# Half tile's expert rows join the joint query and are gathered from the late gather's buffers, on a one-core Trainium2 decoder step

## The chip, the cores and the metric

The kernel runs on one core of a Trainium2 chip, as one program in one launch. The metric is device time in microseconds, the median of several executions. Engines are named as in the profile: PE multiplies matrices (PEld loads its weights), DVE, ACT and POOL work elementwise, SP only issues DMAs. POOL and ACT issue DMAs too; every gather from a table by indices is issued by POOL.

## The reference, cut to what matters

One decoder layer runs over 1024 prompt tokens and 64 sample tokens with the same weights: a norm, one input projection, two token mixers (a retention and an RWKV-7 scan), an output projection, then PEER, an expert mixer, then a gated per-layer embedding and a final norm. PEER is the part that the change touches. Each token queries 8 heads with two halves of 128 keys each, keeps 16 of each half, adds them to candidates, keeps 16 of these, and reads 16 rows per head from two tables of 16384 experts:

```
q = (xb @ wq).reshape(PEER_BLOCK, PEER_HEADS, 2, PEER_DKEY // 2)
s = jnp.einsum('phcd,hcnd->phcn', q, keys).astype(jnp.float32)
sv, si = lax.top_k(s, PEER_TOPK)
cand = sv[:, :, 0, :, None] + sv[:, :, 1, None, :]
cv, ci = lax.top_k(cand.reshape(...), PEER_TOPK)
e = (take(si[:, :, 0], ci // PEER_TOPK) * PEER_NKEYS + take(si[:, :, 1], ci % PEER_TOPK))
gsm = jax.nn.softmax(cv, axis=-1)
hval = jnp.einsum('pd,phkd->phk', xb, u_tab[e])
act = (jax.nn.gelu(hval, approximate=False) * gsm).astype(xb.dtype)
return jnp.einsum('phk,phkd->pd', act, v_tab[e])
```

## The kernel before, in words

The 1088 tokens are cut into nine tiles: tiles 0 to 7 hold 128 prompt tokens each, tile 8 the 64 sample tokens, so it is half a tile. PEER is done in two ways.

*Gathered tiles.* For tiles 0, 1, 8, 2 and 3 each token's 128 rows of both tables are fetched. `gather` issues one indirect DMA per column of the expert list `eid`, 128 rows of 4 KB, 512 KB (L1154 on POOL). First come the rows of the u table: DVE multiplies a row with the token and sums (L1168). Then gelu and the softmax weight on ACT and DVE, then the rows of the v table: DVE adds weight times row to `gacc` in PSUM (L1182). A full tile takes 128 + 128 calls. Tile 8's two halves of the expert list are laid on 128 partitions, so it takes 64 + 64. `gacc` is one buffer, so gathers follow one another. Early gathers (list `E0`: 0, 1, 8) use a ring of eight or nine row buffers in the pool `early`; late gathers (list `G1`: 2, 3) use five buffers named `grow` in the pool `gat`, which is laid out after the pools of the mixers and of `early` are closed and over their memory.

*Dense tiles.* For tiles 4 to 7 (`G2`, 512 tokens) all 16384 experts are multiplied: `hidden` (L1312 and on) makes u times x for 128 blocks of experts, 24 matmuls each, with operands split into a high and a low part on ACT and POOL (tiles `uh`, `ul`); `gates` writes one-hot weights (`oh`, `pwt`, `wst`); `act` multiplies them; `dense` multiplies with v (`vraw`, `vh`, `vl`, `py`). The first 80 hidden blocks are stored in DRAM while the gates are made, the other 48 are used at once (`dense_fused`), then the stored ones are read back (`dense_stored`).

The stages in order are: input projections; mixers of all tiles (`group_b`, order 1, 8, 2 to 7 after tile 0), with `c_rows` behind each (output projection, residual, norm: the tile's row `xd` that PEER reads); the joint query `c_query` for tiles of `G1` and `G2` (16 blocks of weights, for each a matmul per part, scores, and `pick`, five DVE instructions per tile that keep 16 of 128 scores); the hidden stage; fused dense; stored dense; and `ple`, the final stage, tile by tile, in the order `E0 + G2 + G1`. Tile 3's final stage adds `gacc` directly (L1446).

Beside the mixers runs the generator `early`: tile 0's query of its own (`early_query`, 16 weight blocks of 512 KB, matmuls `epq` at L1232 and L1235, 16 picks, then `topk`; for tiles 1 and 8 the scores go to DRAM and back before the picks) and its gather; tile 1's query and gather; and, stepped along with tile 1's gather once tile 8's row is there, tile 8's query; then tile 8's gather. `topk` turns picks into the expert list: sums of candidates, 8 rounds of maxima and index searches, and 8 rounds of a difference on POOL (`eq`, L1102) and a reduction on DVE (`ef`, L1104).

The order on each engine is made by the framework's scheduler when the program is built: it places ready instructions by the order in which the code emits them, with its own estimate of times, and each engine then runs its list strictly in that order, waiting on semaphores. A gather call whose buffer is not free holds up what stands behind it on POOL.

Of the kernel before, what the change touches and what calls it, by code (L numbers as in the profile page):

```python
# [9 lines left out]
F32 = mybir.dt.float32  # L10
# [3 lines left out]
U32 = mybir.dt.uint32  # L14
AF = mybir.ActivationFunctionType
# [156 lines left out]
PWS = 4  # L172
NPRE = 80
NF = 4
TK1 = {2: 1, 3: 4}
GEB = 2
GHB = 2
WQ = 32
# [1 line left out]
WB = 2  # L180
AB = 8
CRING = 4
E0 = [0, 1, 8]
G1 = [2, 3]
DW = 4
LW = 3
CN = 4
# [9 lines left out]
G2 = [4, 5, 6, 7]  # L197
# [3 lines left out]
QB = 4  # L201
SB = 3
EB = 150
SIZE = {t: (64 if t == 8 else 128) for t in range(9)}


def spans(tiles):

    e = [sum(SIZE[t] for t in tiles[:i]) for i in range(len(tiles) + 1)]
    return dict(zip(tiles, e)), e[-1]  # L210
# [8 lines left out]
class K:  # L219
# [797 lines left out]
    def c_query(self, wp, da, parts):  # L1017

        nc, I = self.nc, self.I
        for hc in range(16):  # L1020
            kT = wp.tile([128, 128], F32, name="keysT")
            nc.sync.dma_start(kT, I['keysT'][:, hc])
            raw = da.tile([128, 8, 128], F32, name="wqr", tag="uraw", bufs=UB)
            nc.sync.dma_start(raw, I['wq'][hc])
            wh = da.tile([128, 8, 128], F32R, name="wqh", tag="uh", bufs=DW)
            wl = da.tile([128, 8, 128], F32R, name="wql", tag="ul", bufs=LW)
            self.split(wh, wl, raw, "g")
            for tiles, x in parts:
                off, n = spans(tiles)
                s = wp.tile([128, len(tiles), 128], F32, name=f"ss{tiles[0]}", bufs=SB)  # L1030
                p = self.ps("pq", "b")
                self.mm3(p[:, :n], lambda k: wh[:, k, :], lambda k: wl[:, k, :], lambda k: x[0][:, k], lambda k: x[1][:, k], 8)
                qT = wp.tile([128, n], F32, name=f"qT{tiles[0]}", bufs=1)
                nc.scalar.activation(qT, p[:, :n], AF.Copy)
                p = self.ps("psc", "a")
                for i, t in enumerate(tiles):
                    nc.tensor.matmul(p[:SIZE[t], i * 128:i * 128 + 128], qT[:, off[t]:off[t] + SIZE[t]], kT, start=True, stop=True)
                nc.scalar.activation(s, p[:, :len(tiles) * 128].rearrange("p (t k) -> p t k", k=128), AF.Copy)
                for i, t in enumerate(tiles):
                    self.pick(self.found[t], hc, s[:, i], 128)  # L1040
            yield

    def pick(self, found, hc, s, n):
# [8 lines left out]
    def topk(self, tp, t, s=None, tags={}, ce=None):  # L1052
        nc = self.nc
        n = SIZE[t]
        if s is None:
            sv, si = self.found[t]
        else:
            sv = tp.tile([128, 16, 16], F32, name="sv")
# [47 lines left out]
        if t in G2:  # L1106
            gsm = self.gsm[t] = tp.tile([128, 128], F32, name="gsm", bufs=2)
            self.e12[t] = tp.tile([128, 2, 128], F32, name="e12", bufs=2)
        elif t == 8:
            gsm = tp.tile([128, 128], F32, name="gsm8", tag="cf")  # L1110
        else:
            gsm = self.gsm[t]
        ex = tp.tile([128, 8, 16], F32, name="ex")
# [137 lines left out]
    def early(self, wp):  # L1251

        rows = ("V", "V", "Wq", "Wq", "Wq", "Wq", "W", "xy")
        self.wide = True
        yield from self.early_query(wp, E0[0], "Wq", QB, (("W",), ("xy",)))
        g = self.gather(wp, E0[0], rows, acc=self.acc)
        while E0[1] not in self.rowed:
            next(g, None)
            yield
        self.wide = False  # L1260
        for i, _ in enumerate(self.early_query(wp, E0[1], "Wq", QB, ("Wq", "xT"))):
            if i % 3 == 0:
                next(g, None)
            yield
        yield from g
        g = self.gather(wp, E0[1], rows, acc=self.acc)
        q = None
        for i, _ in enumerate(g):
            yield
            if E0[2] in self.rowed and q is None:  # L1270
                q = self.early_query(wp, E0[2], "Wq", QB, ("Wq", "xT"))
            if q and i % 1 == 0:
                next(q, None)
        for _ in q:
            yield
        self.wide = False
        yield from self.gather(wp, E0[2], rows + ("xT",), acc=self.acc)

    def gates(self, wp, t, extra):
        nc = self.nc  # L1280
# [201 lines left out]
    def build(self):  # L1482
        PS = bass.MemoryType.PSUM
        run = lambda g: [None for _ in g]
        sb = lambda name, es, **kw: self.pool(name, es=es, reuse_waits="tile", **kw)
        with self.es:
# [32 lines left out]
            for _ in a:  # L1519
                for _ in range(IE):  # L1520
# [7 lines left out]
            parts = [G1, G2]  # L1528
            self.layout(cq, [(f"ss{g[0]}", [128, len(g), 128], F32, SB) for g in parts] +
                        [(f"qT{g[0]}", [128, spans(g)[1]], F32, 1) for g in parts])  # L1530
            c1 = sb("cx1", ew, side="right")
            x1 = self.rows_of(c1, G1)
            cx = sb("cx2", ex)
# [1 line left out]
            da = sb("dna", eg, bufs=2)  # L1535
            self.layout(da, [("uh", [128, 8, 128], F32R, DW), ("ul", [128, 8, 128], F32R, LW), ("uraw", [128, 8, 128], F32, UB), ("spare", [128, 8, 128], F32, 1)])
            tp = sb("tk", et)
            self.found = {t: (tp.tile([128, 16, 16], F32, name=f"sv{t}"), tp.tile([128, 16, 16], U32, name=f"si{t}")) for t in G1 + G2}
            self.e12 = {}
            n3 = spans(G2[:-1])[1]  # L1540
            query = self.c_query(cq, da, [(G1, x1), (G2, x)])
# [16 lines left out]
            run(ahead)  # L1558
            run(last)
            run(query)  # L1560
            run(early)
            ew.close()
            ee.close()
# [10 lines left out]
            with ExitStack() as e:  # L1574
# [9 lines left out]
                for i, t in enumerate(G2 + [None]):  # L1584
# [8 lines left out]
                    gate = self.gates(gw, t, da) if t is not None else gate  # L1593
                    for t in G1:
                        if i == TK1[t]:
                            run(self.topk(tp, t))
                            run(self.behind(self.gather(gp, t, acc=acc), PG))
            et.close()
            self.first = True
# [31 lines left out]
```

## Time and profile before

| | |
|---|---|
| runs shown | 3690.5, 3701.82, 3702.95 us (median 3701.82) |
| profiled execution | 3682.12 us, its span 3680.3 us |
| busy over the span | PE 89%, PEld 74%, DVE 78%, ACT 33%, POOL 64% |
| gather calls | 1152, 604 MB of the 1075 MB moved |
| gather of tile 8 | 1863 to 2271 us |
| gather of tile 2, of tile 3 | 2271 to 2934 us, 2934 to 3649 us |

The page's first part gives busy time by engine. Its second part cuts the span into 40 slices with the clock that PE was granted and the busy share of the DMA engines. A table of stretches gives the same for any stretch, and can be restricted to one tile's instructions, which counts the gather calls. A row of a group reads: line, engine, operation, what is written from what, shapes, count, then busy time and mean duration in ns, then the engine's idle time just before and what ended it. A row of the timeline reads: start, duration, engine, line, operation, names, count.

The names in the rows: `Z` is the start of a mixer tile's triangular solve, which PE carries on with the products trz, pG and pZG; `wql` is the low part of a weight block of the joint query, `ul` that of a hidden block, `vl` that of a dense block; `nrs` and `frs` are the two norms of a tile's final stage.

### The profile page before, as it was taken

The page shows a single profiled execution, that of the slowest core. Times are in us where ns is not written, and L with a number is a line of the kernel's source. Part 1 is how long each engine was busy: PE and PEld are TensorE (multiplying, and loading weights), DVE is VectorE, ACT ScalarE, POOL GpSimd, SP SyncE. Part 2 cuts the span into 40 slices and gives each one's busy share as a digit, 9 for nine tenths or more (in the row PEclk, how much of TensorE's full clock was granted, in tenths as well). Part 3 has the DMA queues.
Part 4 walks back from the last instruction along what each step waited for, and adds up shares of the span by engine and source line. Part 5 has one row for each costly group of instructions (what it writes and reads, how often), then busy time and mean ns, then how long its engine had stood idle before and what let it go on. Part 6 is the DMA issues. An engine that isn't in the chain of part 4 may idle for free. (4 is left out here: it accounts for less than half of the span.)

```text
span 3680.3 us, 52362 instructions
## 1 busy us (share of the span) xinstructions
PE 3268.2 (89%) x17749; PEld 2715.5 (74%) x17749; DVE 2857.6 (78%) x5655; ACT 1218.4 (33%) x2259; POOL 2345.1 (64%) x2068
## 2 busy tenths in 40 slices
PE   8798996887968888876989999999999998899988
PEld 7697995654846667655877887887888877667766
DVE  4544689897797886688997999776777787778887
ACT  4233221111211211112333887773333333333322
POOL 5352677554355654436468777768888878887752
PEclk9798996666968885877999999999999999999999
DMA  7257599889858887878678988999999999999974
GB/s 263 86 192 244 200 350 316 277 300 309 280 187 308 311 298 238 300 252 295 206 261 310 324 311 287 345 350 355 342 346 339 332 364 353 369 361 365 340 246 167
DMA packets 423558, 1074.69 MB, mean 292 GB/s; under 512 B 46267, under 2 KB 143289, under 8 KB 418618
## 3 DMA queue, kind: packets, MB, share of 16 engines
q0 software_dynamic: 165888, 604.05, 45.9%
q1 hardware_dynamic: 202670, 377.02, 30.9%
q10 hardware_dynamic: 54732, 90.26, 6.6%
q8 instruction: 141, 2.31, 0.3%
q14 instruction: 127, 1.04, 0.1%
HBM read 980.93 MB, written 90.18 MB: 291 GB/s over the span
## 5 line engine op out<-in xcount | busy, mean ns | idle before, releaser
L1154 POOL DMA_INDIRECT grow<-in_pv,eid x576 | 569.5, 989 | 534.4 <-DVE gacc L1182 299.0
L1154 POOL DMA_INDIRECT grow<-in_pu,eid x576 | 564.2, 979 | 343.1 <-DVE grow L1168 203.2
L1168 DVE SCALAR_TENSOR_TENSOR grow<-grow,gacc 128x1024 f32<-128x1024 f32 x576 | 690.2, 1212 | 116.7 <-DMA grow<-in_pu,eid 114.9
L1182 DVE SCALAR_TENSOR_TENSOR gacc<-grow,ac,gacc 128x1024 f32<-128x1024 f32 x571 | 731.1, 1280 | 33.2 <-DMA grow<-in_pv,eid 28.2
L1353 PE MATMUL py<-ah,vh 128*128 128x512 f32 x1024 | 406.8, 398 | 32.2 <-ACT vh L304 32.2
L333 PE MATMUL ph<-cx,uh 128*128 128x512 f32 x1024 | 406.8, 397 | 7.2 <-DVE al L306 4.6
L334 PE MATMUL ph<-cx,uh 128*128 128x512 f32 x1024 | 405.0, 396 | 0.0
L1354 PE MATMUL py<-al,vh 128*128 128x512 f32 x1024 | 404.7, 395 | 0.0
L308 POOL TENSOR_TENSOR vl<-vraw,vh 128x640 fp32r<-128x640 f32 (+1 forms) x224 | 325.9, 1461 | 39.9 <-ACT vh L304 30.2
L308 POOL TENSOR_TENSOR ul<-uraw,uh 128x1024 fp32r<-128x1024 f32 x128 | 308.1, 2407 | 49.1 <-ACT uh L304 21.0
L1356 PE MATMUL py<-ah,vl 128*128 128x512 f32 x1024 | 272.3, 397 | 13.9 <-POOL vl L308 13.8
L336 PE MATMUL ph<-cx,ul 128*128 128x512 f32 x1024 | 263.4, 395 | 0.0
L1353 PEld LDWEIGHTS py<-ah,vh 128*128 128x128 f32 x1024 | 196.0, 191 | 82.0 <-ACT vh L304 40.3
L304 ACT ACTIVATE vh<-vraw 128x640 fp32r<-128x640 f32 (+1 forms) x224 | 154.8, 692 | 274.3 <-DMA vraw<-in_pvd 95.9
L1356 PEld LDWEIGHTS py<-ah,vl 128*128 128x128 f32 x1024 | 192.3, 189 | 63.3 <-POOL vl L308 21.7
L333 PEld LDWEIGHTS ph<-cx,uh 128*128 128x128 f32 x1024 | 194.8, 190 | 47.0 <-DVE al L306 5.0
L1360 DVE TENSOR_TENSOR yT<-yT,py 128x512 f32<-128x512 f32 x216 | 147.5, 684 | 102.1 <-PE py L1356 101.0
L1354 PEld LDWEIGHTS py<-al,vh 128*128 128x128 f32 x1024 | 195.8, 191 | 41.1
L334 PEld LDWEIGHTS ph<-cx,uh 128*128 128x128 f32 x1024 | 194.5, 190 | 38.5
L336 PEld LDWEIGHTS ph<-cx,ul 128*128 128x128 f32 x1024 | 191.3, 189 | 38.2
L304 ACT ACTIVATE uh<-uraw 128x1024 fp32r<-128x1024 f32 x128 | 135.0, 1056 | 162.0 <-DMA uraw<-in_puT 109.3
L1297 DVE TENSOR_TENSOR oh<-csta,pit 128x1024 f32<-128x1024 f32 x128 | 153.6, 1210 | 27.5 <-ACT oh L1299 17.9
(402 smaller groups left out, 7247.9 us busy)
## 6 DMA issues: line engine op xcount, KB each, us to landing
uraw<-in_puT SPq DMA_DIRECT2D x128, 512.0 KB, 4.2
vraw<-in_pvd SPq DMA_DIRECT2D x128, 320.0 KB, 7.2
cw<-in_w_out SPq DMA_DIRECT2D x128, 256.0 KB, 5.9
wd<-wst ACTq DMA_DIRECT2D x28, 1024.0 KB, 12.3
wt<-wd SPq DMA_DIRECT2D x64, 448.0 KB, 6.8
wraw<-in_w_ret SPq DMA_DIRECT2D x48, 512.0 KB, 4.2
ewq<-in_wq SPq DMA_DIRECT2D x48, 512.0 KB, 5.0
vraw<-in_pvd SPq DMA_DIRECT2D x96, 256.0 KB, 5.4
```

The source lines that it names most:

```text
L304: nc.scalar.activation(hi, src, AF.Copy)
L308: nc.gpsimd.tensor_tensor(lo, src, hi.bitcast(F32), op=OP.subtract)
L333: mm(out, lh(k), rh(k), start=first and k == 0, stop=False)
L334: mm(out, *((ll(k), rh(k)) if right else (lh(k), rl(k))), start=False, stop=False)
L336: mm(out, *((lh(k), rl(k)) if right else (ll(k), rh(k))), start=False, stop=last and k == nk - 1)
L1154: nc.gpsimd.indirect_dma_start(out=g, out_offset=None, in_=src, in_offset=bass.IndirectOffsetOnAxis(ap=self.eid[t][:, j:j + 1], axis=0))
L1168: nc.vector.scalar_tensor_tensor(g[:, c], g[:, c], 1.0, x[:, c], op0=OP.mult, op1=OP.mult, accum_out=hv[:, i, j:j + 1])
L1182: nc.vector.scalar_tensor_tensor(y[:, c], g[:, c], ac[:, j:j + 1], y[:, c], op0=OP.mult, op1=OP.add)
L1297: nc.vector.tensor_tensor(oh, io, p[:, 0:2, s + b:s + b + 4, None].to_broadcast([128, 2, 4, 128]), op=OP.is_equal)
L1353: nc.tensor.matmul(p, vh[:, b, :], ah, start=b == 0, stop=False)
L1354: nc.tensor.matmul(p, vh[:, b, :], al, start=False, stop=False)
L1356: nc.tensor.matmul(p, vl[:, b, :], ah, start=False, stop=b == nb - 1)
```

## The change

The lists change: tile 8 leaves `E0` and goes to the front of `G1`. So `early` ends with tile 1's gather and holds no query for tile 8; the joint query's first part has 320 columns (tiles 8, 2, 3) where it had 256, with one more copy of scores on ACT and 16 more picks of 64 partitions on DVE; `topk` of tile 8 is emitted right behind the joint query, ahead of what is left of `early`; tile 8's gather is emitted in the hidden stage's first round (`TK1` has 8: 0), behind the first 16 hidden blocks, and takes the five buffers of `gat`. Tile 8's picks are kept in a small pool of their own that closes with the mixers' pools. In the final stage tile 8 comes after tiles 4 to 7.

```diff
-TK1 = {2: 1, 3: 4}
+TK1 = {8: 0, 2: 1, 3: 4}
-E0 = [0, 1, 8]
-G1 = [2, 3]
+E0 = [0, 1]
+G1 = [8, 2, 3]
...
-                nc.scalar.activation(s, p[:, :len(tiles) * 128].rearrange("p (t k) -> p t k", k=128), AF.Copy)
+                m = len([t for t in tiles if t == 8])
+                for t in tiles[:m]:
+                    nc.scalar.activation(s[:64, 0], p[:64, :128], AF.Copy)
+                nc.scalar.activation(s[:, m:], p[:, m * 128:len(tiles) * 128].rearrange("p (t k) -> p t k", k=128), AF.Copy)
                 for i, t in enumerate(tiles):
-                    self.pick(self.found[t], hc, s[:, i], 128)
+                    self.pick(self.found[t], hc, s[:, i], SIZE[t])
...
-            gsm = tp.tile([128, 128], F32, name="gsm8", tag="cf")
+            gsm = tp.tile([128, 128], F32, name="gsm8", tag="gsm", bufs=2)
...
         g = self.gather(wp, E0[1], rows, acc=self.acc)
-        q = None
-        for i, _ in enumerate(g):
-            yield
-            if E0[2] in self.rowed and q is None:
-                q = self.early_query(wp, E0[2], "Wq", QB, ("Wq", "xT"))
-            if q and i % 1 == 0:
-                next(q, None)
-        for _ in q:
-            yield
         self.wide = False
-        yield from self.gather(wp, E0[2], rows + ("xT",), acc=self.acc)
+        yield from g
...
+            cf = sb("cf8", ew, side="right")
...
-            self.found = {t: (tp.tile([128, 16, 16], F32, name=f"sv{t}"), tp.tile([128, 16, 16], U32, name=f"si{t}")) for t in G1 + G2}
+            self.found = {}
+            for t in G1 + G2:
+                fp = cf if t == 8 else tp
+                self.found[t] = (fp.tile([128, 16, 16], F32, name=f"sv{t}"), fp.tile([128, 16, 16], U32, name=f"si{t}"))
...
             run(query)
+            run(self.topk(tp, 8))
             run(early)
...
                         if i == TK1[t]:
-                            run(self.topk(tp, t))
+                            if t != 8:
+                                run(self.topk(tp, t))
                             run(self.behind(self.gather(gp, t, acc=acc), PG))
```

The scheduler moves the instructions. How many gather calls stand in POOL's list between marks is, before and in the change:

| between | before | change |
|---|---|---|
| Z of the last mixer tile but one, and Z of the last | 50 | 34 |
| Z of the last mixer tile, and the joint query's first wql | 43 | 39 |
| first wql, first ul | 44 | 44 |
| first ul, first vl | 204 | 188 |
| first vl, last ul | 187 | 189 |
| last ul, last vl | 201 | 200 |
| behind the last vl | 45 | 80 |

Three places of the lists follow. The first is PE's list in the solve of the last mixer tile but one, where tile 8's query (`epq`) stood. Before:

```order
L850 MATMUL trz<-csta,Z 128x128 x4
L855 MATMUL pG<-Z,N 128x64 x4
L862 MATMUL pZG<-G_12122,Tt_12115 128x64 x3
L1232 MATMUL epq<-exT,ewq 128x64 x8
L458 MATMUL tr<-csta,qv 128x128 x4
L862 MATMUL pZG<-G_12122,Tt_12115 128x64
L862 MATMUL pZG<-G_12176,Tt_12169 128x64 x4
L1235 MATMUL epq<-ekT,eqT 64x128
L1232 MATMUL epq<-exT,ewq 128x64 x8
```

In the change, the same solve:

```order
L850 MATMUL trz<-csta,Z 128x128 x4
L458 MATMUL tr<-csta,qv 128x128 x4
L855 MATMUL pG<-Z,N 128x64 x4
L458 MATMUL tr<-csta,qv 128x128 x4
L862 MATMUL pZG<-G_11643,Tt_11636 128x64 x4
L466 MATMUL pin<-qkT 128x128 x8
L862 MATMUL pZG<-G_11669,Tt_11662 128x64 x4
L850 MATMUL trz<-csta,Z 128x128 x4
```

The query's 144 matmuls are gone from between the solve's steps, and the next tile's first products stand there.

The second place is POOL's list at the end of the joint query. `eid_65` is tile 1's expert list, `eid_66` tile 8's. Before:

```order
L308 TENSOR_TENSOR wql<-wqr,wqh 128x1024
L1154 DMA grow<-in_pv,eid_65 128x1024 x2
L308 TENSOR_TENSOR wql<-wqr,wqh 128x1024
L1154 DMA grow<-in_pu,eid_66 128x1024 x3
L308 TENSOR_TENSOR ul<-uraw,uh 128x1024
L1154 DMA grow<-in_pu,eid_66 128x1024 x5
L308 TENSOR_TENSOR ul<-uraw,uh 128x1024
```

In the change, the last calls of tile 1 and the first of tile 8 stand some rows further on, behind tile 8's top-k and the 14th ul:

```order
L1157 DMA grow<-in_pv,eid_65 128x1024
L1105 TENSOR_TENSOR eq<-eid,cf 64x800
L308 TENSOR_TENSOR ul<-uraw,uh 128x1024
L1105 TENSOR_TENSOR eq<-eid,cf 64x800
L308 TENSOR_TENSOR ul<-uraw,uh 128x1024
L1105 TENSOR_TENSOR eq<-eid,cf 64x800
...
L1082 TENSOR_TENSOR eid<-sf 128x8x3
L1085 TENSOR_TENSOR eid<-sf 128x8x6
L1089 TENSOR_TENSOR eid<-sf 128x8x8
L1157 DMA grow<-in_pu,eid_66 128x1024 x5
L308 TENSOR_TENSOR ul<-uraw,uh 128x1024
```

Tile 8's gather followed tile 1's without a gap; now its top-k and the start of tile 4's stand between, with five hidden blocks and no call.

The third place is the end of POOL's list, with the last gather calls of tile 3 (`eid_68`). Before:

```order
L299 TENSOR_TENSOR nrs<-nrs,halves 128x1
L298 TENSOR_SCALAR frs<-fssq 128x1
L1154 DMA grow<-in_pv,eid_68 128x1024
L299 TENSOR_TENSOR frs<-frs,halves 128x1
L1154 DMA grow<-in_pv,eid_68 128x1024
L298 TENSOR_SCALAR frs<-fssq 128x1
L299 TENSOR_TENSOR frs<-frs,halves 128x1
L298 TENSOR_SCALAR nrs<-nssq 128x1
L299 TENSOR_TENSOR nrs<-nrs,halves 128x1
```

In the change:

```order
L298 TENSOR_SCALAR frs<-fssq 128x1
L1157 DMA grow<-in_pv,eid_68 128x1024
L299 TENSOR_TENSOR frs<-frs,halves 128x1
L1157 DMA grow<-in_pv,eid_68 128x1024 x26
L298 TENSOR_SCALAR nrs<-nssq 128x1
L299 TENSOR_TENSOR nrs<-nrs,halves 128x1
L298 TENSOR_SCALAR frs<-fssq 128x1
L299 TENSOR_TENSOR frs<-frs,halves 128x1
```

The calls ended among the norms of the final stage; now 26 stand in a row behind the norms of all other tiles, and only tile 3's two norms come after.

## The prediction

> **What bounds the kernel now.** I read first the table of stretches (busy time of each engine, granted clock, DMA share), cut where the work changes: two ordinary mixer tiles, the tile beside which tile 8's query runs, the rest of the mixers, the joint query, the hidden stage with its gates, fused dense, stored dense, and the final stage in two pieces.
>
> ```profile
> core 0: us, PE busy (x) PEld busy (x) DVE busy (x) ACT busy (x) POOL busy (x), PEclk, DMA share, GB/s
> 1205.00:1305.00 100.00, 84.25 (x513) 65.81 (x514) 84.18 (x161) 18.48 (x37) 58.71 (x58) 0.86 0.88 309
> 1305.00:1407.00 102.00, 88.45 (x509) 70.82 (x509) 81.18 (x157) 18.51 (x37) 55.93 (x57) 0.78 0.82 289
> 1407.00:1589.00 182.00, 149.53 (x812) 122.68 (x812) 120.61 (x269) 29.88 (x74) 72.22 (x71) 0.70 0.75 253
> 1589.00:1708.00 119.00, 91.11 (x476) 67.33 (x474) 93.53 (x177) 19.97 (x35) 54.26 (x60) 0.77 0.87 305
> 1708.00:1860.00 152.00, 145.30 (x880) 129.52 (x881) 147.67 (x635) 47.38 (x79) 89.01 (x67) 0.97 0.68 221
> 1860.00:2502.00 642.00, 604.67 (x3124) 512.50 (x3123) 541.43 (x1182) 431.87 (x870) 486.88 (x386) 0.98 0.88 318
> 2502.00:2953.00 451.00, 451.00 (x1978) 372.30 (x1977) 340.51 (x452) 142.43 (x212) 386.15 (x312) 1.00 0.96 341
> 2953.00:3511.00 558.00, 511.88 (x2146) 408.26 (x2145) 442.68 (x722) 202.71 (x333) 438.63 (x366) 0.97 0.99 355
> 3511.00:3649.00 138.00, 128.29 (x585) 101.42 (x584) 121.95 (x147) 34.94 (x67) 67.72 (x74) 0.95 0.72 240
> 3649.00:3680.00 31.00, 20.95 (x92) 16.14 (x91) 13.84 (x21) 6.22 (x11) 2.23 (x6) 0.95 0.13 51
> ```
>
> The bound changes along the span. The mixers go by a chain over PE and DVE; the joint query by DVE (147.67 of 152 us) with PE close behind; the hidden stage and fused dense by PE (604.67 of 642; 451 of 451); stored dense by DMA (0.99). The last stretch tells who ends the program:
>
> ```profile
> 3647.27 1.28 DVE L1182 SCALAR_TENSOR_TENSOR gacc<-grow,ac,gacc 128x1024 f32<-128x1024 f32 x1
> ...
> 3650.39 1.21 DVE L1446 TENSOR_TENSOR ph<-ph,gacc 128x1024 f32<-128x1024 f32 x1
> ...
> 3659.29 1.42 DVE L1479 SCALAR_TENSOR_TENSOR fin<-ph,frs,row_norm_final 128x512 f32<-128x512 f32 x2 [1.15 <-POOL frs L299]
> ...
> 3675.67 1.41 DVE L1479 SCALAR_TENSOR_TENSOR fin<-ph,frs,row_norm_final 128x512 f32<-128x512 f32 x2 [2.19 <-POOL frs L299]
> ```
>
> The last gathered row of tile 3 is added at 3648.55; its final stage begins at 3650.39 and ends the program; the tile before it is done at 3660.7. So PE's stages and the gather arrive together. Time saved before the dense stages is kept only if the gather arrives as much earlier. I therefore count gather calls per stretch, and compare with where the new order puts them.
>
> ```profile
> core 0: us, POOL busy (x), PEclk, DMA share, GB/s
> 1305.00:1407.00 102.00, 39.04 (x40) 0.78 0.82 289
> 1407.00:1589.00 182.00, 50.59 (x51) 0.70 0.75 253
> 1589.00:1708.00 119.00, 42.14 (x44) 0.77 0.87 305
> 1708.00:1860.00 152.00, 42.39 (x44) 0.97 0.68 221
> 1860.00:2502.00 642.00, 194.41 (x205) 0.98 0.88 318
> 2502.00:2953.00 451.00, 178.54 (x188) 1.00 0.96 341
> 2953.00:3511.00 558.00, 192.68 (x202) 0.97 0.99 355
> 3511.00:3649.00 138.00, 50.38 (x45) 0.95 0.72 240
> ```
>
> By POOL's new order the same stretches hold 34 calls (tile with the query; 50 in the old order), 39 (43), 44 (44), 188 (204), 189 (187), 200 (201), and after the last vl split 80 where 45 stood. PE's stages keep their density of calls; what the shorter mixers and the later start of tile 8 leave over, 35 calls, moves behind the dense stages.
>
> **The change part by part.**
>
> *Query beside the mixers, removed.* The groups of 1407 to 1589 show its PE work.
>
> ```profile
> L1232 PE MATMUL epq<-exT,ewq 128*128 128x64 f32 x256 | 40.1, 321 | 5.4 <-ACT Pi L743 4.7 <-ACT sg L728 0.7
> L1235 PE MATMUL epq<-ekT,eqT 128*64 128x128 f32 x32 | 8.2, 345 | 0.7 <-ACT eqT L1234 0.6
> ```
>
> That is 48 us, some 51 with its transposes. But the tile took 182 us where its neighbours take 100 and 102: the query also stands in PE's queue ahead of the tile's solve chain, and its 16 picks stood on DVE ahead of it. I take the difference to the neighbour, 182 - 102 = 80. Next stretch: tile 8's top-k leaves it and 43 calls become 39; at 119 / 43 = 2.8 us that is 11 at most, 0 at least, 5 taken. Together -85, bounds -51 (only PE's own work) and -115 (34 calls at the neighbour's 102 / 40 = 2.55 us make 87, so -95, and 39 x 2.55 = 99, so -20). SP's queue loses 34 loads (16 of weights at 512 KB, 16 of keys, two of the scratch scores), ACT's eight stores; DMA stood at 0.75 beside them, so their absence is no gain of its own.
>
> The Trainium skill, "TensorE: Matmul & The Clock Gate", Part 1 on the clock gate, says that the clock is throttled by default and PE's activity releases it; by that rule a mixer stretch without the filler matmuls runs colder. The row with the query has 0.70, those without 0.86 and 0.78, the other way round; by the rule, holding 0.70 without it would stretch 88 us of PE work to about 99 and give back some 10 of the 85. I leave it out.
>
> *Joint query, 16 more picks.* Groups of 1708 to 1860:
>
> ```profile
> L1182 DVE SCALAR_TENSOR_TENSOR gacc<-grow,ac,gacc 128x1024 f32<-128x1024 f32 x43 | 54.5, 1266 | 2.1 <-DMA grow<-in_pv,eid 2.0
> L1047 DVE FIND_INDEX8 si<-sv,ss 128x8 uint32<-128x128 f32 x74 | 19.8, 275 | 0.0
> L1048 DVE MATCH_REPLACE8 ss<-sv,ss 128x128 f32<-128x128 f32 x74 | 19.5, 266 | 0.0
> L1046 DVE MAX8 sv<-ss 128x8 f32<-128x128 f32 x78 | 17.8, 267 | 0.0
> ```
>
> A pick is two maxima, two index searches and one replacement: 2 x 267 + 2 x 275 + 266 = 1350 ns laid end to end. They overlap: 147.67 - 54.5 leaves 93 us, with small other work, for about 74 picks, at most 1.26 each. 16 x 1.2 = +19, bounds +11 and +22. The low one is PE's share: 64 more columns in 384 matmuls, at 451 / 1978 = 0.228 us per mostly 512-column matmul, 0.028 each. The extra ACT copies hide under ACT's 47 of 152; without that cover they would cost some 4 us.
>
> *Tile 8's top-k, now in front of its gather.* Its dear parts are eight reductions on DVE and eight differences on POOL:
>
> ```profile
> L1104 DVE TENSOR_REDUCE ef<-eq 64x16 f32<-64x800 f32 x8 | 7.8, 971 | 2.4 <-POOL eq L1102 2.4
> L1102 POOL TENSOR_TENSOR eq<-eid,cf 128x800 f32<-128x800 f32 x48 | 74.0, 1541 | 12.3 <-DVE ef L1104 10.8 <-ACT cf L1097 0.6 <-PE pwt L1302 0.4
> ```
>
> With the small ones, about 18 us of DVE and 16 of POOL enter the hidden stage, and 16 gather calls leave it (16 x 1.27 = 20 of DVE, 16 x 0.95 = 15 of POOL). PE has 605 of 642 us of work there, unchanged. I take 0, bounds -15 and +20. The loss side: in POOL's queue the first calls for tile 8 wait for its expert list to come back by DMA, and the splits for `hidden` stand behind them; three ul buffers cover PE. Where that cover is short, each us waited is a us of PE.
>
> *Dense stages.* 389 calls against 388, same PE work: 0. So the last vl split comes 85 - 19 = 66 us earlier.
>
> *The final stage.* Eight tiles took from 3511 to 3660.7, with some of the last tile's work in between: 146 now, with 51 additions of gathered rows among them (the old 45 all lay there). DVE's order then has 29 additions with nothing beside them, then tile 3 alone. No row shows five buffers at work with nothing beside them. Bounds for one call: the addition itself, 1.28, and fused dense, 451 / 188 = 2.4.
>
> ```profile
> L1182 DVE SCALAR_TENSOR_TENSOR gacc<-grow,ac,gacc 128x1024 f32<-128x1024 f32 x571 | 731.1, 1280 | 33.2 <-DMA grow<-in_pv,eid 28.2
> L1154 POOL DMA_INDIRECT grow<-in_pv,eid x576 | 569.5, 989 | 534.4 <-DVE gacc L1182 299.0 <-issue 43.3 <-DVE si L1047 28.5
> grow<-in_pv,eid POOLq DMA_INDIRECT x45, 5.8
> ```
>
> A buffer's round is 0.99 (issue) + 5.8 (median landing, in the final stage) + 1.28 = 8.1 us, a fifth of it 1.6; I take 1.7, so 29 x 1.7 = 49 (bounds 37 and 70). Tile 3 alone: 3680 - 3651 = 29. From the last vl split to the end 146 + 49 + 29 = 224 against 169: +55, bounds +43 and +76.
>
> The Trainium skill, "DMA: Bandwidth & Descriptors", "Anatomy of one DMA — SWDGE (gpsimd) path", gives 2.0 us plus bytes / 436 GB/s, an estimate of 3.2 us for these 512 KB; the landing row has 5.8 beside other traffic. By the rule the round is 5.5 us, a fifth below DVE's 1.28, and the tail +43 instead of +55.
>
> **Sum**: -85 + 19 + 0 + 0 + 55 = -11 us, against the profiled execution (span 3680.3, own time 3682.1). That lies 19.7 below the median of the runs shown, 3701.8; I carry the difference over: **3691 us**, own range -30 to +12, 3672 to 3714. About 0.5%, 18.5 us, is what a measurement here can tell from no change, so the likeliest is no change to be told: the mixers' gain is handed back by the gather at the end.
>
> **Rivals.**
>
> *Faster: the mixers fall to the gather's own pace and the tail to DVE's.* -95 - 20 + 19 + 43 = -53: 3649. For it: POOL's queue holds only 34 and 39 calls there; landings may shorten with DMA idle. Against: the neighbours' 100 us was PE's and DVE's chain (84 of 100 busy each), which loses nothing.
>
> *Slower: the gather paces everything from its later start.*
>
> ```profile
> 1863.25 1.03 ACT L1162 ACTIVATE gacc<-gx 128x1024 f32<-128x1024 f32 x1
> 1956.50 2.41 POOL L308 TENSOR_TENSOR ul<-uraw,uh 128x1024 fp32r<-128x1024 f32 x1
> ```
>
> Tile 8's gather began at 1863.25, as the query ended. Now it stands behind the 14th ul split, which is the second row; 66 us earlier that is 1890, and with the list's trip about 1897, 34 later than before. If the three late gathers again take 1785 us (1863 to 3648), the end is +34: 3736. It decides as soon as PE waits in fused dense. For it: DMA at 0.96 to 0.99 over 1009 us. Against: PE is never idle in fused dense, with as many calls as it will have.
>
> *The mixers don't close up* (the change doesn't do what it says): only PE's own 51 us are saved, -51 + 19 + 55 = +23: 3725. For it: PE was busy 150 of the 182 us. Against: the cadence of 100 and 102 at every other late tile.
>
> **How the numbers follow.** Forecast 0.46, faster rival 0.22, gather-paced 0.20, mixers 0.12. Faster by over 0.5%: most of the faster rival and a third of the forecast's own range, 0.35. Slower: most of the gather-paced one, half of the last, 0.25. Within: 0.40. The range 3648 to 3738 leaves out half of the faster rival and half of the gather-paced one.
>
> **What would show it.** The tile after 1407 at about 102 us; the joint query at about 171; the last vl split near 3445; 29 additions in a row on DVE behind the last other tile's final stage, at 1.6 to 1.8 us each, with PE idle beside them. Wrong if PE's idle time grows in the hidden stage or in fused dense, or if the tile keeps over 130 us.

## The result, and the profile after

The changed kernel took 3660.84 us (median of 6 runs, 3656.26 to 3679.14), the kernel before 3699.44 us in the same comparison (6 runs, 3690.5 to 3718.47). The ratio is 0.990, 95% interval 0.987 to 0.993: faster by 1.0%. The profiled execution took 3659.46 us, its span is 3657.7, against 3680.3 before: 22.6 less.

The table of stretches for the changed kernel, cut at the same places as before (next to last mixer tile, last mixer stretch, joint query, hidden stage with its gates, fused dense, stored dense, and the final stage in three pieces). Columns: window, its length, busy time and instructions of each engine, granted clock, DMA share, GB/s.

```profile
core 0: us, PE busy (x) PEld busy (x) DVE busy (x) ACT busy (x) POOL busy (x), PEclk, DMA share, GB/s
1420.00:1517.00 97.00, 88.61 (x514) 71.23 (x514) 76.51 (x119) 20.59 (x39) 50.82 (x50) 0.80 0.85 293
1517.00:1624.00 107.00, 87.78 (x478) 65.58 (x479) 79.01 (x100) 21.04 (x36) 49.13 (x51) 0.82 0.90 320
1624.00:1790.00 166.00, 158.20 (x885) 137.22 (x884) 159.11 (x736) 49.42 (x92) 81.09 (x63) 0.97 0.61 204
1790.00:2426.00 636.00, 605.57 (x3156) 512.01 (x3154) 530.80 (x1233) 433.70 (x877) 485.16 (x385) 0.99 0.85 308
2426.00:2876.00 450.00, 449.60 (x1972) 371.30 (x1973) 339.04 (x487) 140.75 (x210) 386.29 (x314) 1.00 0.97 343
2876.00:3428.00 552.00, 516.50 (x2161) 411.49 (x2160) 443.38 (x728) 204.80 (x336) 436.85 (x365) 0.97 1.00 360
3428.00:3576.00 148.00, 132.90 (x598) 103.48 (x596) 126.93 (x156) 36.08 (x68) 74.67 (x82) 0.95 0.75 247
3576.00:3626.00 50.00, 0.00 (x0) 0.00 (x0) 42.19 (x35) 1.15 (x2) 27.01 (x30) 0.52 0.88 317
3626.00:3658.00 32.00, 17.53 (x68) 13.67 (x68) 9.17 (x13) 4.70 (x8) 1.49 (x4) 0.77 0.05 17
```

Two rows tell the story. The tile that took 182 us takes 97, with 514 matmuls where 812 stood (the profile shows each of the query's 144 matmuls as two). And there is a new row, 3576 to 3626, in which PE does nothing at all while DVE is busy 42 of 50 us. The groups of that stretch (busy time and mean of one, then the idle time ahead of them and what ended it) name the work:

```profile
L1185 DVE SCALAR_TENSOR_TENSOR gacc<-grow,ac,gacc 128x1024 f32<-128x1024 f32 x32 | 41.2, 1289 | 7.8 <-DMA grow<-in_pv,eid 6.7 <-DVE gacc L1185 0.4
L1157 POOL DMA_INDIRECT grow<-in_pv,eid x28 | 26.5, 947 | 16.9 <-DVE gacc L1185 14.2 <-issue 1.6 <-DMA grow<-in_pv,eid 1.1
```

These are the additions of tile 3's gathered rows, one behind the other. The gather's calls by stretch show where they came from (POOL's busy time with calls, and their number):

```profile
core 0: us, POOL busy (x), PEclk, DMA share, GB/s
1420.00:1517.00 97.00, 34.47 (x35) 0.80 0.85 293
1517.00:1624.00 107.00, 38.16 (x40) 0.82 0.90 320
1790.00:2426.00 636.00, 178.35 (x188) 0.99 0.85 308
2426.00:2876.00 450.00, 179.16 (x189) 1.00 0.97 343
2876.00:3428.00 552.00, 190.53 (x200) 0.97 1.00 360
3428.00:3626.00 198.00, 86.81 (x80) 0.84 0.79 265
```

Stage by stage, from mark to mark in the two profiled executions (the stretches above, with their ends exact to a tenth):

| stage | before | after | difference |
|---|---|---|---|
| up to the tile beside which the query ran | 1407.2 | 1420.2 | +13.0 |
| that tile | 182.3 | 96.9 | -85.4 |
| rest of the mixers | 118.6 | 106.6 | -12.0 |
| joint query | 152.1 | 165.9 | +13.8 |
| hidden stage | 642.4 | 636.8 | -5.6 |
| fused dense | 451.0 | 449.5 | -1.5 |
| stored dense | 557.9 | 551.5 | -6.4 |
| last vl split to the end | 168.9 | 230.2 | +61.3 |

The first row is work that the change leaves as it was, and the engines' lists are the same there but for two instructions moved. Over the twelve profiled executions here whose program is the same up to that mark it lies between 1398 and 1428, so the +13 is one execution against another. From that mark on the change saves 35.8 us, close to the 38.6 between the medians. Spans of single executions below carry this scatter too; where it matters, the time from that mark on is given.

### The profile page after: what moved, and what is told of

Its sections match the earlier page's. It is cut to its first block, busy times and chain, and to the rows that moved or that the text cites. A ratio compares the mean times of both kernels' runs of the same rounds, so it can differ in the third digit from the quotient of the medians.

```text
span 3657.7 us, 51709 instructions
## 1 busy us (share of the span) xinstructions
PE 3246.3 (89%) x17493; PEld 2693.0 (74%) x17493; DVE 2834.8 (78%) x5655; ACT 1215.8 (33%) x2247; POOL 2336.7 (64%) x2068
```

## The experiments

Stage times below are read at the same marks, from the profiled execution of each kernel.

**Who ends the program: e1 and e2.** The last 35 calls of tile 3 with their additions are left out, once in the changed kernel and once in the kernel before.

```
 in gather(), both kernels
-        for j in range(n):
+        m = n - 35 if t == 3 else n
+        for j in range(m):
...
-            if j < n - 1:
+            if j < m - 1:
```

> The changed kernel without the last 35 of tile 3's 128 rows of the v table (its sum lacks them). Theory, the gather ends the program and hands back most of what the mixers saved: the 29 additions that stood alone at the end go, so the end comes 45 to 60 us earlier than with the change, near 3610 us of span, and from the last vl split to the end it takes about 170 us again. Rival, the final stage is held by PE or DVE work of the tiles and the additions only fill its gaps: within 15 us of the change.

> The kernel before without the last 35 of tile 3's 128 rows of the v table. Theory, PE's stages and the gather arrived together before: only the last tile's final stage moves up, 10 to 25 us. Rival, the gather alone set the end before as well: 35 calls at about 2.4 to 3 us, so 80 us or more earlier.

Measured: e1 3595.74 us (ratio to the kernel before 0.975, 0.972 to 0.978), span 3597.5, 60 below the change's. e2 3676.85 us (0.997, 0.995 to 1.000), span 3673.2, only 7 below. The end of e1, in the table of stretches:

```profile
3426.00:3566.00 140.00, 130.40 (x596) 101.58 (x595) 122.99 (x150) 35.48 (x67) 67.01 (x74) 0.98 0.73 239
3566.00:3598.00 32.00, 19.45 (x79) 14.68 (x78) 12.08 (x18) 6.27 (x11) 2.21 (x6) 0.86 0.10 36
```

The stretch without PE is gone and its 50 us with it. By the medians e2 is 12 us below the kernel before, and so it is from the mark on; both theories held, e2's narrowly. So before, PE and the gather arrived within 7 to 12 us of each other, and in the changed kernel the gather is some 60 us late. With those rows left out of both kernels, the change is worth 3673.2 - 3597.5 = 75.7 us of span (81 between the medians of e2 and e1); with them, 22.6 (38.6 between the medians). This is where about half of the mixers' gain went.

**The two halves of the change: e3 and e4.** e3 has the joint query but gathers tile 8 from the early ring, as before; e4 keeps tile 8's own query beside the mixers but gathers from the late gather's buffers.

```
 e3, against the change
-TK1 = {8: 0, 2: 1, 3: 4}
+TK1 = {8: 9, 2: 1, 3: 4}
...
         yield from g
+        yield from self.gather(wp, 8, rows + ("xT",), acc=self.acc)

 e4, against the kernel before
-        yield from self.gather(wp, E0[2], rows + ("xT",), acc=self.acc)
...
+                    if i == 0:
+                        run(self.behind(self.gather(gp, 8, acc=acc), PG))
```

> The change with one part undone: tile 8's query stays in the joint query, but its gather runs behind tile 1's from the early gather's ring of eight and more row buffers. Theory, only the query's place counts: within 12 us of the change (its list of calls on POOL differs by 1 to 5 calls at each mark). Rival, the five late buffers set the gather's pace in the hidden stage: 25 us or more faster than the change.

> The other part alone: tile 8 keeps its own query beside the mixers, as before, and is gathered from the late gather's five buffers. Theory: as the kernel before, within 15 us, with the tile beside the query at about 180 us. Rival, the buffers are what the gain comes from: 25 us or more faster than before.

Measured: e3 3659.68 us (0.993, 0.991 to 0.995), span 3654.6, the tile 97.3 us and the end 232.3: the change in all but the buffers, within 3 us of it. e4 3669.81 us (0.995, 0.992 to 0.998), span 3678.6, the tile 179.2: stage by stage the kernel before. Its median lies 19 us below that of the kernel before, a little beyond the 15 us that were expected, while its profiled execution is 1.8 below; what makes the median lower stays open. So the short tile and the long end come with the query's place, not with the buffers. How the gain of the whole time divides is less sure: in this comparison e3 is 0.7% faster than the kernel before and e4 0.5%, and the intervals of their ratios overlap.

**The calls placed earlier: e5 and e6.** If the lone additions at the end are the loss, the gathers could be begun sooner: all three in the first round of the hidden stage (e5). e6 does the same to the kernel before.

```
 e5, against the change
-TK1 = {8: 0, 2: 1, 3: 4}
+TK1 = {8: 0, 2: 0, 3: 0}

 e6, against the kernel before
-TK1 = {2: 1, 3: 4}
+TK1 = {2: 0, 3: 0}
```

> The change with the late gathers of tiles 2 and 3 (and their top-k) emitted in the hidden stage's first round, as tile 8's, so that their calls stand further forward: on POOL 214 calls instead of 188 between the first ul and the first vl, 48 instead of 80 behind the last vl, none alone at the end. Theory, the tail of 29 lone additions is what hands the gain back: if PE's stages keep their length, 45 to 60 us faster than the change, span near 3605. Rival, the gather is bound by DMA and DVE in the hidden stage, and calls put there lengthen it by as much: within 15 us of the change.

> The same emission in the kernel before (tiles 2 and 3 in the first round). There PE's stages and the gather arrived together and none of the additions stood alone at the end, so theory: within 15 us of the kernel before. Rival, an earlier emission is a gain by itself, with or without the change: 25 us or more faster than before.

Measured: e5 3679.96 us (0.995, 0.992 to 0.998), span 3666.5, 9 above the change's, and 20 above it from the mark on. e6 3701.85 us (1.0055, 1.002 to 1.009), 12 us slower than the kernel before, inside the 15 that were expected. The theory of e5 fell. In e5 the lone additions are gone and the end takes 179.5 us instead of 230.2, but the hidden stage takes 687 us and not 637, fused dense 10.5 more, stored dense 6.5 more.

```profile
1782.00:2469.00 687.00, 624.81 (x3110) 524.67 (x3109) 572.17 (x1281) 431.63 (x873) 505.02 (x410) 0.95 0.87 307
...
1782.00:2469.00 687.00, 202.64 (x214) 0.95 0.87 307
```

The first row is the hidden stage of e5, the second its gather calls: 214, where the change has 188. So 26 more calls go with 50 us. But the edit moves the top-k of tiles 2 and 3 forward as well, and e6 shows that the calls alone don't set the price: its hidden stage took 665 us instead of 642 with 209 calls instead of 204. In the eleven profiled executions that leave the top-k of tiles 2 and 3 in its place and store 80 hidden blocks, the stage took 632 to 646 us with 179 to 205 calls. The waits of PE in the hidden stage, of e5 and then of the change (what is waited for, us in total, times, longest), show one way in which e5 loses the time:

```profile
PE pwt L1296 <- ACT oh L1293: 26.7, 19, 4.7
PE pwt L1296 <- ACT wst L1297: 14.0, 13, 2.1
PE ph L333 <- ACT uh L304: 11.1, 9, 3.3
PE ph L336 <- POOL ul L308: 8.5, 6, 2.5
```

```profile
PE pwt L1296 <- ACT wst L1297: 9.1, 8, 3.2
PE pwt L1296 <- ACT oh L1293: 6.2, 4, 2.1
PE ph L333 <- ACT uh L304: 5.3, 4, 2.5
PE ph L336 <- POOL ul L308: 4.5, 3, 2.5
```

In these rows PE waits 60 us in e5 and 25 in the change; more than half of the difference is for the gates' one-hots, which DVE starts and ACT completes. With 26 more additions (33 us) and the earlier top-k DVE may come to them later; which of the two it is was not told apart. PE's idle time grew by 32 of the 50 us (687 less 624.81, against 636 less 605.57). The other 19 are PE's own busy time, for about as many matmuls, at a granted clock of 0.95 instead of 0.99. So gathers and their lists could not be put at the head of the hidden stage for nothing, though DVE is at 83% in it and POOL at 74%.

**The lone pace: e7.** Four row buffers in place of five, in the changed kernel.

```
-GBUF = 5
+GBUF = 4
```

> The change with four row buffers for the late gather instead of five. On POOL 674 calls stand before the first vl (683 with the change), 861 before the last ul (872), 1033 before the last vl (1072), and 66 additions stand alone at the end (29). Theory, a lone call takes a buffer's round divided by the buffers, so about 2.0 us instead of 1.7, and 66 of them 130 us instead of 49: 70 to 100 us slower than the change. Rival, DVE's addition or DMA sets the lone pace: 66 at 1.7 us, 112 us, so 50 to 65 us slower.

Measured: 3712.79 us (1.0055, 1.003 to 1.008), span 3718.5, 61 above the change's. DVE's and POOL's groups of the stretch in which PE is idle, now 3569 to 3687:

```profile
L1185 DVE SCALAR_TENSOR_TENSOR gacc<-grow,ac,gacc 128x1024 f32<-128x1024 f32 x66 | 85.1, 1289 | 32.5 <-DMA grow<-in_pv,eid 31.6
...
L1157 POOL DMA_INDIRECT grow<-in_pv,eid x63 | 59.7, 947 | 53.9 <-DVE gacc L1185 44.6 <-DMA grow<-in_pv,eid 9.0 <-issue 0.3
```

66 additions stand alone instead of 32: with one buffer less, fewer calls stand beside the dense stages, and that is the loss, 118 us of lone tail for 50; stored dense, with 172 calls beside it instead of 200, gave 20 us back (531 for 551.5). The pace of one rises from 49.0 / 31 = 1.58 us with five buffers (first to last start) to 116.3 / 65 = 1.79 us with four. A round of fixed length shared by the buffers would give 1.58 x 5/4 = 1.98. So the number of buffers counts for half of what that rule gives and does not set the pace by itself; the loss is the rival's 50 to 65 us; a round shortens from 7.9 to 7.2 us with fewer calls under way, and DVE alone would need 1.29 of the 1.58.

**What the query cost its tile: e8, e9 and e12.** All three are the kernel before with a lighter query for tile 8: a quarter of its weight matmuls (e8), that and two of its sixteen picks (e9), or no loads, the operands on TensorE being a constant already there (e12).

```
 e8
-            for k in range(8):
-                nc.tensor.matmul(p[:, :n], w[:, k], xT[:, k, :n], start=k == 0, stop=k == 7)
+            nk = 2 if t == 8 else 8
+            for k in range(nk):
+                nc.tensor.matmul(p[:, :n], w[:, k], xT[:, k, :n], start=k == 0, stop=k == nk - 1)

 e9, besides
-            for hc in range(16):
+            for hc in range(2 if t == 8 else 16):

 e12, alone
+            if t == 8:
+                kT = self.c("ident")
+            else:
...
-                nc.tensor.matmul(p[:, :n], w[:, k], xT[:, k, :n], start=k == 0, stop=k == 7)
+                nc.tensor.matmul(p[:, :n], self.c("ident") if t == 8 else w[:, k], xT[:, k, :n], start=k == 0, stop=k == 7)
```

> The kernel before with 2 of the 8 weight matmuls per block in tile 8's own query (its scores are wrong, everything else runs, the weights are loaded whole). That takes 192 of 256 matmuls, some 30 us of PE, out of the tile that took 182 us. If the query costs by PE's time and its place in PE's list, the tile falls to 135 to 155 us. If it costs by its loads, picks and top-k, it stays within 10 us of 182. If it costs both ways, between.

> The kernel before with tile 8's own query beside the mixers cut to 2 of 8 matmuls per block and to 2 of its 16 picks (the other 14 are copies; its scores and lists are wrong, weight loads, scratch trips and top-k run whole). The tile beside the query took 182 us, 167 with the matmuls alone cut, 97 without the query. If matmuls and picks are the cost, the tile falls to 100 to 125 us. If the loads, the trip of the scores through DRAM or the place in the lists are, it stays above 145.

> The kernel before, but tile 8's query loads no weights and no keys: its 128 key and weight operands on TensorE are the constant identity, so the scores of tile 8 are not the reference's and the 32 loads of 16 heads are left out; all its matmuls, copies, picks and its place in the order stay. Theory, that what stands on SyncE's queue behind the query's loads (some 33 + 23 us of waits) makes most of the 65 us that matmuls and picks did not explain: the tile falls from 182 to 115 to 140 us and the whole time by 20 us or less, since the gather does not start earlier than the query ends. Rival, that the query's steps hold up the tile where they stand in TensorE's and ScalarE's order (each copy waits for its matmuls, and the next matmul for the copy), loads or not: the tile keeps 165 to 182 us.

Measured: e8 3681.53 us (0.999, 0.996 to 1.001), the tile 167.5 us, between its two cases. e9 3656.92 us (0.994, 0.991 to 0.998), the tile 163.4. e12 3686.62 us (0.999, 0.995 to 1.003), the tile 194.9: without any load it is no shorter. Two theories fell here, that the matmuls and picks were nearly all of it (e9 would have come to 100 to 125), and that SyncE's queue, standing behind the query's loads, was the rest (e12 would have come to 115 to 140; it came out above the 165 to 182 of its rival too). The tile's row of e8, e9 and e12:

```profile
1413.00:1581.00 168.00, 128.06 (x620) 97.88 (x620) 115.03 (x268) 29.71 (x74) 71.07 (x69) 0.67 0.77 263
...
1398.00:1562.00 164.00, 130.40 (x620) 100.54 (x620) 108.00 (x206) 29.75 (x74) 71.53 (x78) 0.67 0.81 276
...
1408.00:1604.00 196.00, 165.07 (x812) 138.43 (x812) 132.73 (x279) 30.07 (x74) 82.44 (x81) 0.64 0.67 220
```

PE's busy time can be parted into the query's matmuls and the others by the groups (in the kernel before 40.1 + 8.2 and 1.4 of transposes; the groups of e9 and e12 are these):

```profile
L1237 PE MATMUL epq<-exT,ewq 128*128 128x64 f32 x64 | 13.3, 346 | 5.9 <-ACT Pi L743 5.0 <-ACT sg L728 0.7 <-PE ewo L622 0.2
L1240 PE MATMUL epq<-ekT,eqT 128*64 128x128 f32 x32 | 7.7, 342 | 0.3 <-ACT eqT L1239 0.3
L1218 PE MATMUL etr<-csta,exn 64*128 64x64 f32 x8 | 1.4, 325 | 0.8 <-ACT N L705 0.8
```

```profile
L1235 PE MATMUL epq<-exT,csta 128*128 128x64 f32 x256 | 46.6, 358 | 0.9 <-ACT Pi L743 0.9
L1238 PE MATMUL epq<-csta,eqT 128*64 128x128 f32 x32 | 9.0, 373 | 0.0
L1214 PE MATMUL etr<-csta,exn 64*128 64x64 f32 x8 | 1.4, 325 | 0.8 <-ACT N L705 0.8
```

| the tile, us | query on PE | other matmuls | PE idle | granted clock |
|---|---|---|---|---|
| before | 49.7 | 99.8 | 32.5 | 0.70 |
| e8, a quarter | 22.0 | 106.1 | 39.9 | 0.67 |
| e9, light | 22.4 | 108.0 | 33.6 | 0.67 |
| e12, no loads | 57.0 | 108.1 | 30.9 | 0.64 |
| after | 0 | 88.6 | 8.4 | 0.80 |

From before to after 85 us: 49.7 of the query itself, 11.2 because the 514 to 516 other matmuls run faster, and 24.1 of idle time. The second part goes with the clock: the other matmuls' time multiplied by the granted clock is 69.9, 71.1, 72.4, 69.2 and 70.9 us, nearly the same in all five. The third part appears as soon as the query's steps stand in the tile, and leaving out the loads, three quarters of the matmuls or seven eighths of the picks does not make it smaller. But it is not the same waiting each time. With all sixteen picks the tile ends in a stretch in which DVE has no gap and PE stands idle for more than half of the time; of the kernel before and of e12:

```profile
1550.00:1589.00 39.00, 16.94 (x46) 11.74 (x46) 38.92 (x154) 1.41 (x5) 15.48 (x14) 0.51 0.50 160
...
1560.00:1604.00 44.00, 18.96 (x75) 13.61 (x73) 43.95 (x164) 3.83 (x11) 21.23 (x21) 0.57 0.57 180
```

What PE waits for in the tile, of the kernel before and then of e9 (us in total, times, longest):

```profile
PE pab L806 <- DVE Q L816: 11.1, 3, 8.3
...
PE ewo L622 <- DMA cw<-in_w_out: 7.7, 5, 2.6
PE pab L806 <- DVE Q L816: 6.0, 3, 3.1
```

So the picks do hold PE up, by way of DVE. Where most of them are left out (e9) this wait is nearly halved, but waits for the weights of the output projection come in, of which the kernel before has none. No run leaves out loads and picks together, so what each is worth of the 24 us stays open, and so do the sixteen pairs of copies on ACT between PE's steps and the 47 to 59 gather calls where the changed kernel has 34.

**A longer early gather, and a lighter hidden stage: e10 and e11.** In the changed kernel tile 8's own query no longer needs the fifth wide buffer, so tile 1's gather can have it (e10). e11 adds to this that only 64 of the hidden blocks are computed ahead and not 80, which leaves the others to fused dense, beside which more calls find place.

```
 e10, against the change
-        g = self.gather(wp, E0[1], rows, acc=self.acc)
-        self.wide = False
+        g = self.gather(wp, E0[1], rows + ("xT",), acc=self.acc)

 e11, besides
-NPRE = 80
+NPRE = 64
```

> The change with one more row buffer for tile 1's gather (the tile xT, free once tile 1's query is done): five instead of four beside the mixers. On POOL 472 calls stand before the joint query instead of 451, 80 instead of 80 less 8 behind the last vl, 21 additions alone at the end instead of 29. Theory, what the gather brings in earlier beside the mixers shortens the lone tail without lengthening PE's stages: 8 x 1.7 = 14 us faster than the change, up to 35 if the 8 calls fewer in the hidden stage show too. Rival, the mixers lengthen by what the tail loses, as the hidden stage did: within 8 us.

> The same, and 64 hidden blocks stored instead of 80, so that 64 instead of 48 are used at once. No addition stands alone at the end in DVE's list. Per block, hidden and stored stages took 637 / 80 + 552 / 80 = 14.9 us of which fewer than 11 are PE's, fused 450 / 48 = 9.4. Theory: hidden stage 637 - 16 x 5.5 = 550, fused 600, stored 441, so 45 us less, and the lone tail's 49 go as well: 70 to 95 us faster than the change. Rival, the hidden stage is held by the gates (ACT and DVE) and doesn't shrink below 600: 20 to 45 us faster.

Measured: e10 3641.60 us (0.990, 0.983 to 0.997), span 3643.9, 14 below the change's, and the stage behind the last vl split is 14.4 shorter, as its theory has it. But the ratio is the change's own, 0.990, and from the mark on e10 takes as long as the change to within 1 us: the last two mixer stretches together, the hidden stage and stored dense are 5, 4 and 8 us longer. A gain of e10 over the change is not shown; the rival, within 8 us, is not excluded. e11 3607.63 us (4 runs, 3596.55 to 3611.77; 0.982, 0.974 to 0.989), span 3594.8. The hidden stage came to 579 us, between the 550 of the theory and the 600 of its rival; fused dense came to 638, where 600 was expected, and stored dense to 458, where 441 was. Its last four stages, and the gather calls in them:

```profile
1759.00:2338.00 579.00, 528.94 (x2722) 449.24 (x2721) 493.05 (x1190) 405.01 (x839) 415.72 (x340) 0.96 0.81 292
2338.00:2976.00 638.00, 638.00 (x2810) 527.20 (x2809) 479.96 (x706) 200.81 (x299) 545.25 (x442) 1.00 0.96 339
2976.00:3434.00 458.00, 420.57 (x1770) 333.09 (x1769) 375.68 (x586) 167.49 (x276) 372.49 (x315) 0.99 1.01 365
3434.00:3595.00 161.00, 144.16 (x661) 113.44 (x659) 125.83 (x159) 41.55 (x78) 57.82 (x74) 0.97 0.59 195
...
2338.00:2976.00 638.00, 253.47 (x268) 1.00 0.96 339
...
3434.00:3595.00 161.00, 40.05 (x39) 0.97 0.59 195
```

Fused dense takes 268 calls and PE is still never idle in it; behind the last vl split 39 remain, and the end takes 160 us instead of 230. The three dense stages together are 1675 us, 37 more than in the change, so net of them the end's 70 is worth 33. Of the 63 us between the spans 34 are there already two tiles ahead of the mark in the first table (1177.1 in e11, 1210.7 in the change), where the order of both programs has hardly begun to differ; so about 30 are the edits', which is the rival's 20 to 45 and not the theory's 70 to 95. The medians of e10 and e11, which ran together, differ by 34, so the gain comes with the 64 stored blocks. This version beats both kernels; the two ratios to the kernel before, 0.982 and 0.990, come from different comparisons.

## Why the prediction was right and where it was wrong

The time was inside the range, which at 90 us is wide enough to hold the kernel before as well, and the order of events was as told. But the likeliest case, no change to be told, was not what came: the kernel is 1.0% faster. By the prediction's own steps:

- **Query beside the mixers, -85.** Measured -97.4: -85.4 for the tile (-80 was taken) and -12.0 for the next stretch (-5 was taken). Taking the neighbour's pace was right, and so was refusing PE's own 51 us (49.7 by the groups) as the measure. The reason given, the query ahead of the solve chain on PE and its picks on DVE, is borne out for the picks in the tile's last 39 us, but it is only part of it: e9 took three quarters of the matmuls and most picks away and the tile kept 163 of its 182 us. The clock, which the prediction left out, goes with 11 us of the others' time.
- **The clock.** With the query the granted clock of this tile was 0.64 to 0.72 in seven profiled executions (the kernel before, e2, e4, e6, e8, e9, e12), without it 0.77 to 0.85 in seven (the change, e1, e3, e5, e7, e10, e11). Leaving a colder tile out was right; taking the rows as they stood, with a gain in it, would have been better. The Trainium skill, "TensorE: Matmul & The Clock Gate", Part 1 on the clock gate, says that PE's activity releases the throttle. The tile's rows do not speak against that sentence, only against the step that the prediction took from it: without the query's matmuls PE was busy for a larger share of the tile (0.91 in the change), not a smaller one, than with them (0.76 to 0.84 in the kernel before, e8, e9 and e12). A stretch of e12 does not fit it: 50 us at half clock with PE busy throughout (last section).
- **Joint query, +19.** Measured +13.8, 0.86 us for each of the 16 picks and not 1.2. DVE is busy 159 of 166 us, so it does bound the stage, but its busy time rose by 11.4 us only: the price of a pick was read too high. Inside the bounds.
- **Tile 8's top-k and the hidden stage, 0.** Measured -5.6. **Dense stages, 0.** Measured -7.9. No run here shows a cause for these few us. The last vl split came at 3427.5, where the prediction said near 3445.
- **Final stage, +55.** Measured +61.3. The additions stand in a row with PE idle, as told, at 1.58 us each. The 49 us for them answer to 50 without PE, but by luck: 32 at 1.58 us stood there and not 29 at 1.7. The rest, 148 + 32 us, was taken as 146 + 29.
- **The price of a lone call.** The Trainium skill, "DMA: Bandwidth & Descriptors", "Anatomy of one DMA — SWDGE (gpsimd) path", led to an estimate of 3.2 us for a landing and 1.28 us for a call. Measured 1.58 us a call: a round of 7.9 us, from which 0.95 of issue and 1.29 of addition leave 5.7. The profile's landing row, 5.8, was the better guide.
- **The sum.** -11 against -22.6 between the two profiled executions, or -35.8 from the place where the programs part. Every stage ahead of the last gave a few us more than taken (5 in the tile, 7 in the mixers' rest, 5 in the joint query, 6 and 8 behind it), together more than the whole of what was forecast; the final stage cost 6 more.
- **The offset, +19.7.** This is the largest miss of the level. The profiled execution of the kernel before was taken as 19.7 us too fast against the median of three runs, and the change was put on the same scale. But the changed kernel's profiled execution (3659.46) is at its median (3660.84), and over the later comparisons the kernel before itself had medians of 3677 to 3690 (78 executions of 3650 to 3724). So the distance belonged to the executions of that comparison (its three others, 3695.65 to 3718.47, were as high) and not to the program. Without the carried offset the same sum gives 3671, 0.3% off.

The rivals. *Faster*, the nearest in time (3649 against 3660.84): the mixers came near its price (-97 of its -115), but the tail did not fall to DVE's pace (1.58 and not 1.28). *Gather from a later start*, 3736: tile 8's gather did begin later, at 1874.0 and not 1863.25, but by 11 us and not 34 (the mark ahead of it came 13 us later in this execution), and the three late gathers took 1752 us instead of 1785, for which the last 32 additions can account in the main, alone at 1.58 us each where fused dense gives a call in 450 / 189 = 2.4. One part of it holds by e1: the gather does end the program. *Mixers don't close up*, 3725: excluded by the tile's 97 us.

## What to carry to other kernels

Where two streams of work arrive together, a gain in one is worth only what the other can follow: price the end of both, and find out who is late, and by how much, by leaving out the last rows of one. Put the work of a lagging stream beside the stage whose bound engine it does not use (in e11 fused dense, made longer, took 268 calls with PE never idle), and don't trust that a stage is free because its engines look so: with gathers and their lists begun at its head the hidden stage lengthened by as much as the lone tail had cost. Do not carry the distance of one profiled execution from a median of three runs into a forecast.

## What the runs showed of the hardware that was not expected

- The granted clock of the mixer tile is lower when the query stands in it (0.64 to 0.72, against 0.77 to 0.85), in the fourteen profiled executions here, and the other matmuls of the tile lengthen in proportion: their time multiplied by the clock is 69 to 72 us in the five that were worked out. It is not a matter of how many matmuls are added (0.67 with 104 in e9, 0.70 with 296), nor of PE's idle time alone. In the kernel before, the half clock of 1550 to 1589, which holds none of the query's matmuls, comes where PE waits for DVE; but in e12 the clock stayed at half through 50 us in which PE had no gap:

```profile
1450.00:1500.00 50.00, 50.00 (x219) 45.48 (x220) 20.66 (x26) 6.87 (x18) 10.63 (x12) 0.50 0.52 164
```

What the clock answers to in such a tile stays open.
- After 50 us in which PE did nothing (granted clock 0.52 in that row) the last tile's final stage took 31.4 us, against 31.8 before, where PE had been busy up to it; the clock in it was 0.77 against 0.95. Before, PE still had some matmuls of the tile ahead to do in that time (92 in the row, against 68), so what the lower clock cost is not told by this pair.
- The lone pace of the gather rises by less than the number of buffers falls (1.58 us with five, 1.79 with four), with DMA at 0.88 and 0.85 of its time in those stretches; whether DMA sets the rest of the pace was not tested.
